# Hybrid encoder layer on one core: the merge-gate columns of the long sequence with seven block products in place of eight, block sums kept in DRAM

## The chip, the cores and the metric

One NeuronCore of a Trainium2 chip runs the whole program in one launch. The metric is the device time in microseconds (us) of that core; lower is better. All tensors are float32. Every matrix product is done in split form: an operand x is written as hi + lo in the chip's float32r type, and a product is three matmuls, hi·hi, hi·lo and lo·hi.

## The reference

Two sequences, 1024 tokens (called 0 below) and 2048 tokens (called 1), of width 1024 pass through one encoder layer; 16 learned meta tokens stand ahead of each.

```python
xn = _rmsnorm(h, g_pre)
proj = xn @ w_in + b_in                    # 1024 -> 6672 columns
na_q, na_k, na_v, na_z, ml_qk, ml_v, ml_z, ml_o, ml_g, mg = jnp.split(proj, SPLIT_IDX, axis=-1)
ya = (neighbourhood_attention(na_q, na_k, na_v, na_rpb) * silu(na_z)) @ w_a
yb = (mlstm_branch(ml_qk, ml_v, ml_g, ml_o, ...) * silu(ml_z)) @ w_b
ga, gb = jnp.split(jax.nn.sigmoid(mg), 2, axis=-1)
y = (ga * ya + gb * yb) @ w_out
return h + _rmsnorm(y, g_post)
```

The change is about `mg`, the last 2048 of the 6672 columns: `sigmoid(xn @ w_in[:, 4624:6672] + b)`.

## The kernel before, in words

**Two streams of work on one TensorE.** `dense` is a generator that yields the big products one small piece at a time, each with its cost; `sparse` is a generator for the mLSTM (`ml`) and the neighbourhood attention (`na`). `run` steps `sparse` and, between its steps, as many pieces of `dense` as the step's number says. TensorE's instruction order is just the order in which Python emits it; the order on the other engines and on the DMA-issuing queue (SyncE, SP) is made by a scheduler at build time. All engines run their own list strictly in order.

**The dense plan.** `PLAN` lists groups (sequence, first token, columns). A group covers 1024 tokens as two halves of 512. Letters: "m" the mLSTM columns, "n" the attention columns, "g" the 16 merge-gate column blocks of 128; ("f", s, b) are the final products. The order is 0m, 0n, 1m at token 0, 1m and 1n at 1024, 1n at 0, then the gates 1g at 0, 1g at 1024, 0g, then six finals. `sparse` runs ml 0, na 0, ml 1, na 1; ml 0 waits until group 0m is done.

**Columns with the weights stationary (`fm_half`).** For one column block of 128 and one half of 512 tokens, 8 k-blocks times three matmuls (`mm3`, lines 170 to 172) of 128x512 go into one PSUM bank of the ring "pj" (three banks). ScalarE and VectorE then read the bank (`fm_evac`; the gates are a tanh, line 530) into a buffer of the ring "st" (four buffers), and a DMA stores it to DRAM. The z columns of "m" take two "st" buffers each (lines 526 to 528). `tm_unit` (lines 607 to 609) does value columns with the tokens stationary.

**Weights.** `wload` brings a raw weight unit of 512 KB (`wraw`, line 242); `wpump` splits it into `whi` and `wlo` (lines 264, 265; four buffers each), and `wflush` stores both parts to DRAM (line 285), from where they come back when the same columns are needed again (line 257).

**x.** The split x of a half (`xh`, `xl`, two buffers each, 4 MB of DMA for both) is built from a transposed copy of the input; halves of sequence 1 that are needed again later are written to DRAM (`xkeep`, `xput`, one 256 KB piece on every fourth turn of `beside`) and reloaded. For sequence 0 the gates group builds x once more.

**The start of the mLSTM (`ml_gates`).** The mLSTM's own gates (`g_t`, loaded from DRAM, line 975) go through a dozen small VectorE and ScalarE steps, ending in `g_lf` (line 995); TensorE then multiplies `g_lf` by a triangle of ones (line 1001). In TensorE's order this stands a little after the last column of group 0m.

Of the kernel before, what the change touches and what calls it, by code (L numbers as in the profile page):

```python
# [40 lines left out]
PLAN = ((0, 0, "m"), (0, 0, "n"), (1, 0, "m"), (1, 1024, "m"), (1, 1024, "n"), (1, 0, "n"), (1, 0, "g"), (1, 1024, "g"), (0, 0, "g"), ("f", 0, 0), ("f", 0, 1), ("f", 1, 0), ("f", 1, 1), ("f", 1, 2), ("f", 1, 3))  # L41
STEPS = (("ml", 0, ()), ("na", 0, (0, 1)), ("ml", 1, ()), ("na", 1, (0, 1, 2, 3)))
# [11 lines left out]
def _weight_units():  # L54

    return ([("i", x, P) for x in FM_COLS] + [("t", *c, a) for c in TM_COLS for a in range(2)]
            + [("m", f, P) for f in range(KT)] + [("o", c, a) for c in range(4) for a in range(2)])

# [63 lines left out]
class K:  # L122
# [3 lines left out]
    def __init__(self, tc, ins, outs):  # L126
# [8 lines left out]
        self.hold, self.early = deque(), True  # L135

# [55 lines left out]
    def gain(self, name):  # L192

        g = self.wp.tile([P, D], F32, name="gain", bufs=1)
        self.nc.sync.dma_start(g, _bc(self.i[name], 0, D))
        return g
# [37 lines left out]
    def wload(self, most=2):  # L234

        while self.wreq and sum(x[1] is not None for x in self.wraw) < most:
            key, src, nk, w = self.wreq.popleft()
            raw = None
            if key not in self.wseen:
                self.wseen.add(key)  # L240
                raw = self.wrp[0].tile([P, 4 * WU], F32, name="wraw", bufs=self.wrp[1])
                self.nc.sync.dma_start(raw[:, :nk * w], src)
            self.wraw.append((key, raw, nk, w))

    def wpump(self, most=NBW, parts=1, copy=None):
# [4 lines left out]
        while self.wraw and self.wout < most:  # L250
# [3 lines left out]
            lo = wp.tile([P, 4 * WU], F32R, name="wlo", bufs=NBW)  # L254
            if raw is None:
# [43 lines left out]
    def rsum(self, xs, res, first=None):  # L299
# [7 lines left out]
        for q, (xr, n) in todo:  # L307
            junk = wp.tile([P, D], mybir.dt.bfloat16, name="xsq", tag="thT", bufs=1)
# [53 lines left out]
    def opening(self, xp):  # L362
# [17 lines left out]
        self.xnext = [self.xtload(0, 512, e, wp, 4) for e in (0, 1)]  # L380
        self.wload(4)
        self.xnext += [self.xtload(0, 512, e, wp, 4) for e in (2, 3)]
# [17 lines left out]
        self.rr = wp.tile([P, 2, 512], F32, name="rr", tag="gain", bufs=1)  # L400
        self.rm = cp.tile([P, NM], F32, name="rm")
        dt = wp.tile([P, HALF], F32, name="dt", tag="thT", bufs=1)
# [5 lines left out]
        self.wrp = wp, 2  # L408
# [9 lines left out]
        self.rwait[0, 0] = rows  # L418

    def build_half(self, s, t0, res):  # L420
# [13 lines left out]
        if s == 0:  # L434
            xts = self.xnext or [self.xtload(s, t0, e, wp, 4) for e in range(4)]
# [6 lines left out]
            if not self.done:  # L442
                p = self.psum("sm", [P, 512])
                nc.tensor.matmul(p[:, :KT], self.ident, g, start=True, stop=True)
                g = self.cp.tile([P, KT], F32, name="gx")
                nc.vector.tensor_copy(g, p[:, :KT])
            x, r = self.xparts(), []
            for e in range(4):
                self.xsplit(x, xts[e], e, 0, g)
                if not self.done:  # L450
                    self.wflush(2)
                yield
            res.append(tuple(x))
            if self.done:
                return
# [4 lines left out]
            def rows():  # L460
                self.rrows(dg, self.rr[:, 1], "sm")
                self.xp.close()
            self.rwait[s, t0] = rows
        else:
            toks, r = self.tokens(s, t0, range(4), wp, 4), []
# [3 lines left out]
            xts = [self.xtload(s, t0, e, wp, 4) for e in range(3)]  # L469
            yield  # L470
            rr = wp.tile([P, 512], F32, name="rx", tag="thT", bufs=1)
            self.rrows(dg, rr, "pj")
            xts.append(self.xtload(s, t0, 3, wp, 4))
# [16 lines left out]
    def xkeep(self, s, t0, x):  # L490
        where = [j for j, g in enumerate(PLAN) if g[:2] == (s, t0 // 1024 * 1024)]
        if where[-1] - where[0] >= len(where):
            self.xkept[s, t0] = []
            for x, part in zip(x, "hl"):
                d = self.dp.tile([P, KT, 512], F32, name=f"x{part}{s}_{t0}")
                self.xput.extend((d[:, k, :], x[:, k, :512].bitcast(F32)) for k in range(KT))
                self.xkept[s, t0].append(d)

    def beside(self):

        self.turn += 1
        if self.xput and self.turn % 4 == 1:
            self.nc.sync.dma_start(*self.xput.popleft())

# [48 lines left out]
    def fm_half(self, col, w, x, s, t0, meta, done=None, tags=None, late=None):  # L553
# [10 lines left out]
        for j, (q, k) in enumerate(order):  # L564
            c0, c1 = chunks[q]
            if q == len(ps):
                ps.append(self.psum("pj", [P, 512]))
            self.mm3(ps[q][:, :c1 - c0], w[0][:, k, :], w[1][:, k, :], x[0][:, k, c0:c1], x[1][:, k, c0:c1],
                     start=k == 0, stop=k == KT - 1)
# [12 lines left out]
    def tm_unit(self, col, halves, wd):  # L582
        nc, wp = self.nc, self.wp
        ws = self.wtake(2)
        bb = wp.tile([P, WU], F32, name="bb", bufs=2)
# [7 lines left out]
        for j, (x, s, c, n, cnt, tok) in enumerate(todo):  # L593
            st = wp.tile([P, 2, WU], F32, name="stT", bufs=4)
# [81 lines left out]

    def requests(self):
# [3 lines left out]
        for j, (s, t0, cols) in enumerate(PLAN):  # L681
# [3 lines left out]
            else:  # L685
                keys = []
                for kind, c in self.layout(cols):
                    if j >= 5 and ahead:
                        keys.append(ahead.popleft())
                    keys += [("i", x, P) for x in c] if kind == "fm" else [("t", *c, a) for a in range(2)]  # L690
            for k in keys:
                nk, w = (KT, P) if k[0] in "im" else (4, k[2] if k[0] == "t" else 256)
# [17 lines left out]

    def group(self, s, t0, meta, cols, reuse, nxt):
# [3 lines left out]
        nb = None  # L715
        for j, (kind, c) in enumerate(jobs):
            if kind == "tm":
# [3 lines left out]
                continue  # L721
            ws = self.wtake(len(c))
            last = j == len(jobs) - 1
# [357 lines left out]
    def conv_load(self, mp, src, c0, n, T):  # L1081
# [3 lines left out]
        raw = mp.tile([P, BL + 2], F32, name="raw", bufs=3)  # L1085
# [22 lines left out]
    def ml(self, s):  # L1108
# [3 lines left out]
        with tc.tile_pool(name=f"mg{s}", bufs=1, side="right", reuse_waits="tile") as keep:  # L1112
            with tc.tile_pool(name=f"mt{s}", bufs=1, side="right", reuse_waits="tile") as mp:
                self.tri = keep.tile([P, 2, P], F32, name="tri")
                nc.sync.dma_start(self.tri, self.i["tri"])
                self.trim = keep.tile([P, 2, CB, P], F32, name="trim")
                for j in range(CB):
                    nc.sync.dma_start(self.trim[:, :, j, :], self.i["trimask"])
                g = []
                yield from self.ml_gates(s, keep, mp, g)  # L1120
            with tc.tile_pool(name=f"ml{s}", bufs=1, side="right", reuse_waits="tile") as mp:
                self.vas = [mp.tile([P, CB, 130], F32, name=f"va{j}") for j in range(3)]
# [32 lines left out]
    def ml_states(self, mp, s, h, g, NB, sts):  # L1155
# [17 lines left out]
        def conv_b(i):  # L1173
            if i < N:
                n, c0 = seq[i]
                th, c = next(convs.pop(i))
                kf = mp.tile([P, BL], F32, name="kf", bufs=3)
# [29 lines left out]
        for i in range(N):  # L1207
# [7 lines left out]
            kth = mp.tile([P, CB, P], F32R, name="kth", tag="kh", bufs=2)  # L1215
            ktl = mp.tile([P, CB, P], F32R, name="ktl", tag="kl", bufs=2)
# [590 lines left out]
```

## Time and profile before

| | |
|---|---|
| time, median of 3 runs | 2741.05 us (2740.09 to 2742.14) |
| the profiled execution: its time, its span | 2741.18 us, 2739.3 us |
| granted TensorE clock | 0.998 |
| TensorE (PE) busy | 2721.4 us, 99% |
| VectorE (DVE), ScalarE (ACT) busy | 65%, 49% |
| DMA | 660.22 MB, mean 241 GB/s |

PE is the matmul side of TensorE, PEld its weight loads, DVE VectorE, ACT ScalarE, SP the queue that issues nearly all DMAs. In the profile the 512-wide matmuls overlap, so a matmul's own duration is longer than the step from one start to the next. A row of the strip view is one digit for each fortieth of the span, about 68.5 us.

### The profile page before, as it was taken

To read this page: it belongs to the slowest core of one execution; us is meant where nothing else is said; L and a number is where in the kernel's file an instruction comes from. 1 tells how busy PE (TensorE), PEld (TensorE's weight loads), DVE (VectorE), ACT (ScalarE), POOL (GpSimd) and SP (SyncE) were. 2 spreads that over 40 slices of the span, in tenths; PEclk is the share of its full clock that TensorE was granted. 3 is DMA by queue.
4 is the path that set the end of the run, shared out by engine and by line. 5 is a ranking of instruction groups with operands and counts; after the bars stand their busy time and mean duration, and the time that the engine had idled before them with its cause. 6 is when DMAs were issued, how large, how long until landed. Compare 5 with 4: busy or idle time off the path is not lost.

```text
span 2739.3 us, 46935 instructions
## 1 busy us (share of the span) xinstructions
PE 2721.4 (99%) x16312; PEld 2399.3 (88%) x16312; DVE 1785.8 (65%) x5042; ACT 1340.8 (49%) x3236; POOL 16.0 (1%) x104
## 2 busy tenths in 40 slices
PE   9999999999999999999999999999999999999998
PEld 7998898899889988978988888888888989989898
DVE  5332688765556655457768667575668798897854
ACT  6212546543454454256456655563555655555521
POOL 0000000000000000000000000000000000000000
PEclk9999999999999999999999999999999999999999
DMA  9644768855875544596766688576559798988965
GB/s 371 243 163 171 253 209 318 283 182 171 322 242 162 168 142 147 179 320 206 266 234 229 243 306 286 196 235 226 186 191 303 234 327 271 330 282 280 323 233 208
DMA packets 362046, 660.22 MB, mean 241 GB/s; under 512 B 46704, under 2 KB 176448, under 8 KB 361808
## 3 DMA queue, kind: packets, MB, share of 16 engines
q1 hardware_dynamic: 360688, 654.52, 70.9%
q0 software_dynamic: 1120, 2.69, 0.5%
q8 instruction: 129, 2.11, 0.3%
q14 instruction: 109, 0.89, 0.1%
HBM read 454.85 MB, written 202.22 MB: 240 GB/s over the span
## 4 chain that ended last, share of the span: by engine, by line
PE 94%; DMA 3%; DVE 1%; ACT 1%; issue 0%; SPq 0%; DVEq 0%; ACTq 0%
PE pj L170 19%; PE pj L172 19%; PE pj L171 19%; PE pj L607 5%; PE pj L608 5%; PE pj L609 5%; PE pj L1587 3%; PE pj L1589 3%; PE pj L1588 3%; PE sm L941 3%; PE tr L926 3%; DMA wraw<-wu 1%; PE sm L172 1%; PE sm L171 1%; PE sm L170 1%; PE sc L894 1%
## 5 line engine op out<-in xcount | busy, mean ns | idle before, releaser
L170 PE MATMUL pj<-xh,whi 128*128 128x512 f32 (+1 forms) x1984 | 782.3, 394 | 0.4 <-ACT whi L264 0.3
L171 PE MATMUL pj<-xl,whi 128*128 128x512 f32 (+1 forms) x1984 | 764.4, 385 | 0.1
L172 PE MATMUL pj<-xh,wlo 128*128 128x512 f32 (+1 forms) x1984 | 764.2, 385 | 0.2 <-DVE wlo L265 0.2
L172 PEld LDWEIGHTS pj<-xh,wlo 128*128 128x128 f32 x1984 | 373.4, 188 | 80.5 <-DVE wlo L265 0.4
L170 PEld LDWEIGHTS pj<-xh,whi 128*128 128x128 f32 x1984 | 373.4, 188 | 67.0 <-ACT whi L264 1.2
L171 PEld LDWEIGHTS pj<-xl,whi 128*128 128x128 f32 x1984 | 374.0, 189 | 64.3 <-issue 1.0
L607 PE MATMUL pj<-whi,xh 128*128 128x256 f32 (+1 forms) x1152 | 329.0, 286 | 0.0
L608 PE MATMUL pj<-wlo,xh 128*128 128x256 f32 (+1 forms) x1152 | 324.8, 282 | 0.0
L609 PE MATMUL pj<-whi,xl 128*128 128x256 f32 (+1 forms) x1152 | 324.6, 282 | 0.0
L1587 PE MATMUL pj<-whi,mh 128*128 128x256 f32 x768 | 220.0, 286 | 0.6 <-DMA whi<-wh 0.6
L607 PEld LDWEIGHTS pj<-whi,xh 128*128 128x128 f32 x1152 | 217.2, 189 | 0.2
L608 PEld LDWEIGHTS pj<-wlo,xh 128*128 128x128 f32 x1152 | 217.0, 188 | 0.1
L609 PEld LDWEIGHTS pj<-whi,xl 128*128 128x128 f32 x1152 | 216.9, 188 | 0.0
L1589 PE MATMUL pj<-whi,mlo 128*128 128x256 f32 x768 | 216.4, 282 | 0.0
L1588 PE MATMUL pj<-wlo,mh 128*128 128x256 f32 x768 | 216.2, 281 | 0.0
L933 DVE TENSOR_TENSOR pts<-tr,pts 96x384 fp32r<-96x384 f32 (+2 forms) x192 | 119.0, 620 | 83.4 <-ACT pts L928 82.0
L928 ACT ACTIVATE pts<-tr 96x384 fp32r<-96x384 f32 (+2 forms) x192 | 103.6, 539 | 127.6 <-PE tr L926 126.7
L170 PE MATMUL pj<-yh,whi 128*128 128x512 f32 x384 | 154.3, 402 | 0.0
L171 PE MATMUL pj<-yl,whi 128*128 128x512 f32 x384 | 151.2, 394 | 0.7 <-DVE yl L1489 0.7
L172 PE MATMUL pj<-yh,wlo 128*128 128x512 f32 x384 | 151.8, 395 | 0.0
L1587 PEld LDWEIGHTS pj<-whi,mh 128*128 128x128 f32 x768 | 145.2, 189 | 1.7 <-DMA whi<-wh 0.8
L1588 PEld LDWEIGHTS pj<-wlo,mh 128*128 128x128 f32 x768 | 145.2, 189 | 0.9
(290 smaller groups left out, 4972.3 us busy)
## 6 DMA issues: line engine op xcount, KB each, us to landing
whi<-wh SPq DMA_DIRECT2D x192, 512.0 KB
wlo<-wl SPq DMA_DIRECT2D x192, 512.0 KB
wraw<-wu SPq DMA_DIRECT2D x64, 512.0 KB
wh<-whi SPq DMA_DIRECT2D x64, 512.0 KB
wl<-wlo SPq DMA_DIRECT2D x64, 512.0 KB
gt<-st SPq DMA_DIRECT2D x96, 256.0 KB
tg<-gt SPq DMA_DIRECT2D x96, 256.0 KB
xt<-xt SPq DMA_DIRECT2D x32, 512.0 KB
```

The costliest lines, as they stand in the source:

```text
L170: mm(out, ah, bh, start=start, stop=False)
L171: mm(out, ah, bl, start=False, stop=False)
L172: mm(out, al, bh, start=False, stop=stop)
L607: nc.tensor.matmul(o, xh, wh, start=k == 0, stop=False)
L608: nc.tensor.matmul(o, xh, wl, start=False, stop=False)
L609: nc.tensor.matmul(o, xl, wh, start=False, stop=k == KT - 1)
L926: nc.tensor.transpose(pt[:ks, ch, :], pr_[:, ch * ks:(ch + 1) * ks], self.ident)
L928: nc.scalar.activation(pts[:ks, :nb, 0, :], pt[:ks, :nb], AF.Copy)
L933: self.nc.vector.tensor_tensor(pts[:ks, :nb, 1, :], pt[:ks, :nb], pts[:ks, :nb, 0, :].bitcast(F32), op=ALU.subtract)
L1587: nc.tensor.matmul(o, mh[:, k, xs], wh, start=clear > 0 and k == 0, stop=False)
L1588: nc.tensor.matmul(o, mh[:, k, xs], wl, start=False, stop=False)
L1589: nc.tensor.matmul(o, ml[:, k, xs], wh, start=False, stop=clear < 2 and k == KT - 1)
```

## The change

For sequence 1 the gates are computed as a 2x2 block product: two column blocks (a pair) by two halves of tokens, over the even and the odd k-blocks. Winograd's form of Strassen's scheme needs seven block products, where the plain way has eight. One block product is 4 k-blocks times three matmuls of 128x512, so a pair costs 84 matmuls, where the plain way costs 96. It is used for all 8 pairs of group 1g at token 0 and for 7 of 8 pairs at token 1024; the first pair there ("lead") and all of sequence 0 stay plain.

- **Weights (`wprep`)**: in group 0m, beside the products, the 16 raw gate units are loaded, four sums are made for each pair, and 8 operands are split and stored to DRAM: 8 pairs x 8 operands x 512 KB. Their SBUF (pool "pq") lies where ml's first pool goes next, and the group's end runs `wprep` out. A product's weights come back as one operand of 512 KB (hi and lo).
- **x (`tprep`)**: in the two groups 1n four token-block sums are made, split and stored to DRAM, 8 MB for each group; three come back into their own SBUF tiles (`tload`; room is made by closing the pool "bp" and opening "gp"), the fourth over the even k-blocks of the second half's x.
- **Products (`sgates`)**: three PSUM banks A, E, R hold the partial sums; ScalarE copies bank to bank, VectorE adds twice for each pair.
- x of sequence 0 is now also written to DRAM in group 0m and reloaded for its gates. The row factors `rr` go to DRAM and back.
- The prefetch of the final weights starts two groups earlier.
- In `ml` some buffers shrink: `raw` and `kf` from 3 to 2, `kh` and `kl` from 2 to 1, `va` from 3 to 2; `s1` shares a buffer with `th`.

```diff
+SW = ((1, 0), (1, 1024))
...
     def beside(self):
         self.turn += 1
-        if self.xput and self.turn % 4 == 1:
+        if self.xput and self.turn % 4 == 1 and self.turn > 48:
             self.nc.sync.dma_start(*self.xput.popleft())
+        if self.side and self.turn % self.pace == 0 and next(self.side, "end") == "end":
+            self.side = None
...
+    def wprep(self):
+        with self.tc.tile_pool(name="pq", bufs=1, side="right", reuse_waits="tile") as pool:
...
+            for p in range(8):
+                raw = raws.pop(p)
+                sm = pool.tile([P, 4, 512], F32, name="ps", bufs=1)
+                todo = [((p, "11"), (p, "12"), raw[:, 0]), ((p, "21"), (p, "22"), raw[:, 1]),
+                        ((p, "s1"), (p, "s2"), sm[:, 0:2]), ((p, "s3"), (p, "s4"), sm[:, 2:4])]
+                for n, (a, b, x) in enumerate(todo):
+                    o = pool.tile([P, 2, 2, 512], F32R, name="po", bufs=3)
+                    nc.scalar.activation(o[:, :, 0], x, AF.Copy)
+                    nc.vector.tensor_tensor(o[:, :, 1], x, o[:, :, 0].bitcast(F32), op=ALU.subtract)
+                    for q, key in enumerate((a, b)):
+                        self.qd[key] = self.dp.tile([P, D], F32, name=f"q{p}{key[1]}")
+                        nc.sync.dma_start(self.qd[key][:, :], o[:, q].rearrange("p a c -> p (a c)").bitcast(F32))
+                    yield
...
+    def sgates(self, s, t0, lead, nxt):
+        for hf in range(2):
+            if hf == 0:
+                ws = [self.wtake(1)[0] for _ in range(2 * len(lead))]
+            for (p, f), w in zip([(p, f) for p in lead for f in range(2)], ws):
+                yield from self.fm_half(C_GA + (2 * p + f) * P, w, self.xs[hf], s, t0 + 512 * hf, False, done=self.wdone if hf else None)
+        pairs = [p for p in range(8) if p not in lead]
+        self.tload(s, t0, (0,))
...
+            if i == 0:
+                yield from prod(A, "11", True)
+                nc.scalar.activation(E, A, AF.Copy)
+            yield from prod(A, "12", False)
+            if end and nxt:
+                nx = [self.xload(*nxt)]
+            yield from prod(E, "s2", False)
+            out(2 * p, 0, new(), A)
+            yield from prod(R, "s3", True)
+            nc.scalar.activation(A, E, AF.Copy)
+            u7 = new()
+            nc.scalar.activation(u7, R, AF.Copy)
+            for op in ("22", "s1") if i == 0 else ("s1", "22"):
+                yield from prod(A if op == "22" else E, op, False)
+            c22, c21 = new(), new()
+            nc.vector.tensor_tensor(c22, E, u7, op=ALU.add)
+            out(2 * p + 1, 1, c22, c22)
+            nc.vector.tensor_tensor(c21, A, u7, op=ALU.add)
+            out(2 * p + 1, 0, c21, c21)
+            if not end:
+                yield from prod(R, "11", True)
+                nc.scalar.activation(A, R, AF.Copy)
+            yield from prod(E, "s4", False)
+            out(2 * p, 1, new(), E)
+            A, E, R = R, A, E
...
     def group(self, s, t0, meta, cols, reuse, nxt):
...
+            if last and sw:
+                self.drain()
+                self.gopen()
+                self.tload(s, t0, (1, 2, 3))
...
     def dense(self, ctx):
...
+            if cols == "g" and (s, t0) in SW:
+                if not same[0]:
+                    self.xs.append(self.xload(s, t0 + 512))
+                    self.tload(s, t0, (1, 2, 3))
+                for cost in self.sgates(s, t0, self.lead(j), nxt and nxt[:2]):
+                    yield cost
+                    self.beside()
...
+            else:
+                yield from self.group(s, t0, meta, cols, same[0], nxt)
+                if self.side:
+                    self.drain()
```

More of the change, by code (lines that the diff above doesn't have):

```diff
@@ L238, in wload @@
             raw = None
-            if key not in self.wseen:
+            if key[0] != "q" and key not in self.wseen:
                 self.wseen.add(key)
@@ L434, in build_half @@
         if s == 0:
[L435 removed]
+            xts = self.xnext
             self.xnext = None
@@ L441, in build_half @@
             g = self.gpre
[L442 to L446, printed above, removed]
+            p = self.psum("sm", [P, 512])
+            nc.tensor.matmul(p[:, :KT], self.ident, g, start=True, stop=True)
+            g = self.cp.tile([P, KT], F32, name="gx")
+            nc.vector.tensor_copy(g, p[:, :KT])
             x, r = self.xparts(), []
```

253 lines of the change are left out of this document (208 added, 45 removed).

## The prediction, on record before the changed kernel was run

> **What bounds the kernel now.** First the page: the span, the busy shares, and the strips of the DMA engines.
>
> ```profile
> span 2739.3 us, 46935 instructions
> PE 2721.4 (99%) x16312; PEld 2399.3 (88%) x16312; DVE 1785.8 (65%) x5042; ACT 1340.8 (49%) x3236; POOL 16.0 (1%) x104
> ...
> DMA  9644768855875544596766688576559798988965
> GB/s 371 243 163 171 253 209 318 283 182 171 322 242 162 168 142 147 179 320 206 266 234 229 243 306 286 196 235 226 186 191 303 234 327 271 330 282 280 323 233 208
> ```
>
> TensorE is busy 99% of the span, everything else much less; the DMA engines are full in the first fortieth (9 tenths, 371 GB/s) and have room after it. "Busy" alone does not say that TensorE never waits, so next the chronological list of its instructions, in the gate stage, and the view of who waited for whom, for TensorE.
>
> ```profile
> 1499.81 0.40 PE L170 MATMUL pj<-xh,whi 128*128 128x512 f32 x1
> ...
> 1500.97 0.39 PE L172 MATMUL pj<-xh,wlo 128*128 128x512 f32 x1
> ```
>
> ```profile
> PE sm L170 <- ACT kth L1217: 3.4, 2, 1.9
> PE sm L171 <- DVE v L1321: 1.9, 2, 1.3
> ```
>
> Five steps lie between the two matmuls: (1500.97 - 1499.81)/5 = 0.232 us for each 128x512 matmul, start to start. The waits are the two longest entries: 3.4 us in two times. So the kernel is TensorE's list of matmuls, end to end. A matmul taken out is worth 0.232 us, and any new wait of TensorE is paid in full, as no slack stands anywhere to absorb it.
>
> **What is taken out.** A pair of column blocks costs 7 x 12 = 84 matmuls of 128x512, where it cost 96; 8 pairs at token 0 and 7 at token 1024 make 15 x 12 = 180 fewer. 180 x 0.232 = 41.8 us. Nothing is added on TensorE. This term is sure.
>
> **What is added in group 0m: 50 MB of DMA where the engines were half full.** In stretches of the first 290 us (columns: stretch, its length, busy us of PE, PEld, DVE, ACT, POOL, granted clock, DMA share, GB/s):
>
> ```profile
> 0.00:20.00 20.00, 18.43 (x102) 14.03 (x103) 11.23 (x26) 14.26 (x26) 0.74 (x10) 1.00 0.88 327
> 20.00:40.00 20.00, 19.92 (x134) 17.78 (x133) 13.09 (x43) 14.95 (x30) 0.10 (x1) 1.00 1.02 410
> 40.00:60.00 20.00, 20.00 (x86) 15.90 (x85) 9.85 (x23) 9.67 (x15) 0.50 (x8) 1.00 1.00 362
> 60.00:80.00 20.00, 20.00 (x88) 16.15 (x87) 6.15 (x20) 7.94 (x15) 0.47 (x9) 1.00 0.95 374
> 80.00:130.00 50.00, 50.00 (x327) 45.86 (x326) 18.50 (x26) 14.99 (x20) 0.00 (x0) 1.00 0.60 205
> 130.00:180.00 50.00, 50.00 (x421) 50.00 (x420) 15.63 (x32) 9.43 (x15) 0.00 (x0) 1.00 0.53 177
> 180.00:230.00 50.00, 50.00 (x392) 48.68 (x391) 11.72 (x25) 7.73 (x13) 0.00 (x0) 1.00 0.44 154
> 230.00:290.00 60.00, 59.65 (x266) 46.88 (x265) 23.80 (x65) 21.11 (x43) 0.10 (x1) 1.00 0.60 213
> ```
>
> When full, the engines move 362 to 410 GB/s; 374 at a share of 0.95 makes 395, which I take. `wprep` loads 16 units of 512 KB and stores 64 operands of 512 KB (8.4 + 33.6 MB), and x of sequence 0 is written out (8.4 MB). In the built program SP's list up to the last operand store has 288 transfers with 114.5 MB. At 395 GB/s these take 290 us, and 3 us more for the slow first stretch (327 in place of 395 for 20 us).
>
> Who waits for that? ml's first pool lies where "pq" was, so one of its first loads waits for the last operand stores, and `g_t` stands behind it on SP, which works strictly in order. TensorE's first use is L1001:
>
> ```profile
> L975 SPq DMA_DIRECT2D g_t<-gg x2: 405/416/428, 158.4 to 1119.9; - x2
> ...
> 167.63 0.22 DVE L995 TENSOR_TENSOR g_lf<-g_lf,g_e 128x72 f32<-128x72 f32 x1
> ...
> L1001 PE MATMUL sm<-g_lf,tri x8: 195/275/279, 262.0 to 1129.9; 128*128 128x36 f32 x4, 128*128 128x68 f32 x4
> ```
>
> Before, `g_t` is issued at 158.4, `g_lf` is ready at 167.8 (9.4 us later) and TensorE comes to it at 262.0: 94 us of slack. After, TensorE's list up to this point is the same, but `g_lf` is ready at 290 + 3 + 9 = 302. TensorE stands **40 us** late there, however the wait is shared out on the way. At 410 GB/s it is 27 (279 + 9.4 - 262), at 362 it is 64 (316 + 9.4 - 262, plus 1).
>
> Most of it should show much earlier, by the "st" buffers:
>
> ```profile
> 62.47 2.17 SPq L537 DMA_DIRECT2D mq<-st  x3
> ...
> 69.48 0.69 ACT L526 ACTIVATE st<-pj,bfm 128x512 f32<-128x512 f32 x1 [2.89 <-DMA mq<-st]
> ```
>
> Already now the first evacuation of the z columns waits 2.9 us for a store of an earlier "st" buffer. In SP's list that store (the first mq of the second half) is at 24.9 MB; in the new list it is at 37.1 MB. 12.2 MB / 395 GB/s = 31 us later, so the evacuation comes at about 100. ScalarE is in order too: everything behind it waits, the operand splits of `wprep` among it, which need one of three "po" buffers whose stores are in the same backlog. TensorE has three "pj" banks: with 24 x 0.232 = 5.6 us for a column and half it runs on to about 75 and then stops for some 24 us, at the fourth z column. The rest of the 40 comes at L1001.
>
> [...]
>
> `wprep`'s own instructions cost nothing:
>
> ```profile
> L265 DVE TENSOR_TENSOR wlo<-wraw,whi 128x1024 fp32r<-128x1024 f32 x61 | 74.5, 1222 | 42.8 <-ACT whi L264 33.8 <-PE sm L329 4.3 <-PE sm L1377 2.7
> L264 ACT ACTIVATE whi<-wraw 128x1024 fp32r<-128x1024 f32 x61 | 64.5, 1060 | 90.5 <-PE pj L171 50.2 <-PE pj L609 26.1 <-DMA wraw<-wu 10.6
> L1554 DVE TENSOR_TENSOR tg<-tg 128x512 f32<-128x512 f32 x48 | 32.8, 683 | 0.5
> ```
>
> 32 splits and 32 sums make 32 x 1.22 + 32 x 0.68 = 61 us of VectorE and 34 us of ScalarE, in a stage where VectorE is busy 46 of 150 us (80 to 230). 16 splits of gate weights go away later. `tprep` is 31 us of VectorE in each group 1n (12 operations of 1.22 and 24 of 0.68 for four parts), with 8 MB of stores: covered as well; where it is not, up to 5 us each.
>
> **The gate stage.** Rows: the tanh of the gates, and two stretches of the stage.
>
> ```profile
> L530 ACT ACTIVATE st<-pj,bfh x96: 667/687/692, 1433.4 to 2068.3; 128x512 f32<-128x512 f32 x96
> ...
> 1433.00:1640.00 207.00, 207.00 (x1036) 173.30 (x1035) 148.77 (x484) 122.47 (x314) 0.70 (x6) 1.00 0.74 258
> 1640.00:1860.00 220.00, 219.35 (x1098) 183.39 (x1097) 151.06 (x500) 125.15 (x330) 0.20 (x2) 1.00 0.71 244
> ```
>
> 96 halves of 24 x 0.232 us are 535 of the 635 us between the first and the last tanh: the share of dense work is 0.84. A product needs 512 KB of weights per 2.8 us of TensorE, where a plain block had 1 MB per 11.1 (or 1.5 MB with raw load and store in the first group). In the built programs the SP bytes of the first gates group go from 59 to 63 MB, of the second from 46 to 61 MB; with 7/8 of the time that is about 0.9 of the engines. So on average they hold, except at the seam between the groups. There the last pair of token 0 is followed by the lead pair of token 1024, whose second half of x can only be loaded when the last product is done, and stands in SP's list behind the first half (4.2 MB), three reloaded sums (6.3 MB), weights, gate stores and ml's loads: 18.6 MB from the start of the first half's load to the piece that TensorE needs first. 18.6 MB / 395 = 47 us. TensorE has 5 products and the lead's two columns to do meanwhile: (5 x 12 + 48) x 0.232 / 0.84 = 29.8 us. It waits **17 us** (16 at 410, 22 at 362; 5 if the sums go out of the way earlier).
>
> The bank copies: each is one ScalarE operation of the size of L530 (0.687 us). All but the first of a group have a product (2.8 us of TensorE) to hide behind; if that cover went, 15 pairs x 0.7 = 10 us. The first stands between "11" and "12" on the same bank: 2 groups x about 1.2 us = **2 us**. ml's smaller buffers still let each load start four or more steps ahead; I take **1 us** for them and `tprep`, 0 to 15 as bounds (below zero nothing, as nothing gets shorter there).
>
> **The sum**, against the profiled execution (2741.18 us; the median of the runs is 2741.05): 2741.2 - 41.8 + 40 + 17 + 2 + 1 = 2759.4, say **2760 us**, slower by 0.7%. A difference under 0.2% (5.5 us) could not be told from none.
>
> **Rivals.**
> - *The matmuls count, the DMA keeps up* (faster). If large rows go out quicker than in any stretch above, or the backlog is worked off beside it, both waits shrink. It decides at 36 us of waits in all; that needs, say, 430 GB/s over the first 266 us (14 us at L1001) and 13 at the seam: 2741.2 - 41.8 + 14 + 13 + 3 = 2729. For it: most new transfers have 4 KB rows. Against: the row of 20 to 40 us is at a share of 1.02 with 410. Chance 0.18, for 2710 to 2735.
> - *Only the start waits*: the seam is covered by what is left in the buffers: 2741.2 - 41.8 + 40 + 3 + 1 = 2743. Against: bytes between the two loads. Chance 0.17.
> - *Waits breed waits*: ml with fewer buffers and VectorE's extra work stall TensorE too (15), and the engines move 362 in place of 395 (24 more at L1001, 5 at the seam): up to 2804. The row of 40 to 60 us is for it, the shares of VectorE are against it. Chance 0.12.
> - *The clock falls.* TensorE at half speed after a long wait: no wait over 1.9 us is in the trace, and the clock is 1.00 in each stretch above, the first with its idle start included. If each of four long waits cost as much as the longest wait seen (1.9 us), 8 us: 2768. Chance 0.05. [...]
>
> The forecast itself, both waits, has 0.48 (2748 to 2785).
>
> **How the numbers follow.** Low end 2722: within the first rival; high end 2792: the middle of the third. What is left out is half of the first rival (0.09) and half of the third (0.06), and some of the spread. Faster by over 0.2%: the first rival, 0.18. Within 0.2%: some half of the second, 0.10. Slower: the rest, 0.72.
>
> **What would show it.** Right: DMA share 0.95 or more from 20 to 290 us; a wait of over 15 us of TensorE between 70 and 110 us with ScalarE idle "<-DMA mq<-st" ahead of L526's counterpart; `g_t` issued near 290 and L1001's counterpart at 295 to 310; TensorE waiting for `xh` or `xl` some 17 us at the seam; 180 fewer matmuls. Wrong: a DMA rate over 420 GB/s in the first 250 us, L1001's counterpart before 285, or a seam without a wait; the error of the sum is then in that term.

## The result, and the profile after

The changed kernel takes 2818.05 us (median of 6 runs, 2814.24 to 2824.64); the kernel before, beside it, 2741.27 us. The ratio is 1.0281, 95% interval 1.0268 to 1.0295: 77 us slower, where the prediction had 2760 us in a range of 2722 to 2792. The profiled execution has a span of 2814.2 us, 74.9 us more than before. The page of the changed kernel:

```profile
span 2814.2 us, 47371 instructions
PE 2703.1 (96%) x16132; PEld 2379.4 (85%) x16132; DVE 1887.8 (67%) x5176; ACT 1394.3 (50%) x3305; POOL 16.3 (1%) x100
...
PEclk9899899999999999999999998999999999999989
DMA  9999666966697756479778889888669798998945
```

The 180 matmuls are gone (16312 - 16132), and TensorE is idle for 111 us in place of 18 (the span less the busy time). Who made it wait, longest first:

```profile
PE pj L185 <- ACT st L627: 23.1, 1, 23.1
PE sm L1233 <- DVE g_lf L1227: 16.1, 1, 16.1
PE pj L185 <- DMA xh<-xh: 15.2, 1, 15.2
PE pj L186 <- DMA xl<-xl: 5.1, 1, 5.1
PE pj L185 <- ACT yh L1742: 5.1, 1, 5.1
PE pj L185 <- ACT st L632: 5.0, 2, 4.0
PE sm L1173 <- ACT prb L1141: 4.9, 3, 3.5
PE sc L1574 <- DVE den L1624: 3.7, 1, 3.7
PE tr L1705 <- DVE hb L1700: 3.7, 1, 3.7
```

Before, the longest entry was 3.4 us. Some of these waits also slow what comes behind them: about the 4.0 us wait the granted clock is 0.50, from 59.7 to 66.5 us. The chronological list of TensorE after it (start, duration, and the idle time before):

```profile
61.53 0.79 PE L185 MATMUL pj<-xh,whi 128*128 128x512 f32 x1 [4.00 <-ACT st L632]
62.12 0.63 PE L186 MATMUL pj<-xl,whi 128*128 128x512 f32 x1
...
66.39 0.46 PE L187 MATMUL pj<-xh,wlo 128*128 128x512 f32 x1
```

From the second row to the last shown are ten steps: (66.39 - 62.12) / 10 = 0.427 us each, where the prediction counted 0.232. Ten such steps cost 10 x 0.195, some 2 us.

To put the loss at places, I took for each pair of matmuls that follow each other the step from start to start, less the median step of the same two widths before. The sums by stage (idle: steps over 0.3 us too long; slow: the rest, some 15 of its 16.2 us in stretches where the granted clock is 0.50):

| stage, us of the changed kernel | before | after | more |
|---|---|---|---|
| group 0m and the mLSTM's first gates, 0 to 400 | 8.5 | 59.7 | 51.2 |
| 400 to 760 | 5.5 | 6.7 | 1.2 |
| x and sums of token 1024, 760 to 1150 | 5.7 | 20.4 | 14.7 |
| sums of token 0, 1150 to 1390 | 10.5 | 19.9 | 9.4 |
| first gates group, 1390 to 1640 | 3.0 | 3.8 | 0.8 |
| the seam, 1640 to 1780 | 1.4 | 26.2 | 24.8 |
| 1780 to 2640 | 16.3 | 12.7 | -3.6 |
| the end of the attention, 2640 to 2815 | 1.9 | 19.6 | 17.7 |
| all | 52.8 | 169.0 | 116.2 (100.2 idle, 16.2 slow) |

116.2 - 41.8 = 74.4, against 74.9 measured. The windows that answer to those shown of before (same columns), with one of VectorE's full stretches:

```profile
20.00:40.00 20.00, 20.00 (x137) 18.15 (x136) 13.46 (x44) 14.99 (x32) 0.11 (x1) 1.00 1.03 405
...
60.00:80.00 20.00, 18.47 (x70) 14.82 (x71) 2.07 (x3) 5.05 (x8) 0.15 (x1) 0.84 0.92 324
80.00:130.00 50.00, 26.94 (x110) 21.42 (x109) 26.83 (x44) 21.89 (x30) 0.10 (x1) 0.76 1.02 410
130.00:180.00 50.00, 49.41 (x390) 48.55 (x389) 25.85 (x37) 16.24 (x21) 0.00 (x0) 1.00 1.03 406
180.00:230.00 50.00, 50.00 (x426) 50.00 (x426) 26.85 (x40) 12.03 (x14) 0.00 (x0) 1.00 1.00 375
230.00:290.00 60.00, 60.00 (x362) 53.48 (x361) 30.35 (x43) 21.88 (x28) 0.00 (x0) 1.00 0.96 361
290.00:350.00 60.00, 43.57 (x206) 34.33 (x205) 27.52 (x79) 24.08 (x54) 0.78 (x13) 0.86 0.61 212
...
1300.00:1320.00 20.00, 16.25 (x75) 13.48 (x75) 19.90 (x43) 14.04 (x34) 0.00 (x0) 0.91 0.79 275
```

The DMA engines are busy at 0.92 or more in every stretch from 20 to 290 us. The first long wait of TensorE lies inside, from 80.8 to 103.9 us: ScalarE can't empty a PSUM bank into a buffer "st" until the stores that SP issued at 92.8 us have read it (SP's and ScalarE's lists):

```profile
92.81 4.06 SPq L637 DMA_DIRECT2D mq<-st  x4
...
102.22 0.69 ACT L626 ACTIVATE st<-pj,bfm 128x512 f32<-128x512 f32 x1 [5.64 <-DMA mq<-st]
```

Right behind the full stretch TensorE loses its second block. In SP's list the end of the backlog and the gate loads behind it, and TensorE's first use (from the views of single lines and tiles):

```profile
L564 SPq DMA_DIRECT2D q7s<-po x4: 319/413/1101, 296.7 to 298.9; - x4
...
L1206 SPq DMA_DIRECT2D g_t<-gg x2: 380/402/423, 304.3 to 1185.7; - x2
...
L1233 PE MATMUL sm<-g_lf,tri x8: 221/341/426, 310.9 to 1197.5; 128*128 128x36 f32 x4, 128*128 128x68 f32 x4
```

### The profile page after: what moved, and what is told of

It reads as the page before. It is cut to its first block, busy times and chain, and to the rows that moved or that the text cites. A ratio compares the mean times of both kernels' runs of the same rounds, so it can differ in the third digit from the quotient of the medians.

```text
span 2814.2 us, 47371 instructions
## 1 busy us (share of the span) xinstructions
PE 2703.1 (96%) x16132; PEld 2379.4 (85%) x16132; DVE 1887.8 (67%) x5176; ACT 1394.3 (50%) x3305; POOL 16.3 (1%) x100
## 4 chain that ended last, share of the span: by engine, by line
PE 84%; DMA 10%; DVE 3%; ACT 1%; SPq 1%; issue 1%; DVEq 0%; POOL 0%; ACTq 0%; POOLq 0%
PE pj L185 12%; PE pj L187 12%; PE pj L186 12%; PE pj L707 5%; PE pj L708 5%; PE pj L709 5%; PE pj L890 3%; PE pj L892 3%; PE pj L891 3%; PE pj L1824 3%; PE pj L1826 3%; PE pj L1825 3%; PE sm L1173 3%; PE tr L1158 2%; DMA xl<-xl 1%; DMA xt<-xt 1%
## 5 line engine op out<-in xcount | busy, mean ns | idle before, releaser
L185 PE MATMUL pj<-xh,whi 128*128 128x512 f32 (+1 forms) x1360 | 535.7, 394 | 46.2 <-ACT st L627 23.1
L186 PE MATMUL pj<-xl,whi 128*128 128x512 f32 (+1 forms) x1360 | 523.0, 385 | 5.5 <-DMA xl<-xl 5.1
L187 PE MATMUL pj<-xh,wlo 128*128 128x512 f32 (+1 forms) x1360 | 521.8, 384 | 3.7 <-DMA wlo<-wl 3.4
L185 PEld LDWEIGHTS pj<-xh,whi 128*128 128x128 f32 x1360 | 258.5, 190 | 92.0 <-ACT st L627 23.5
L187 PEld LDWEIGHTS pj<-xh,wlo 128*128 128x128 f32 x1360 | 258.2, 190 | 58.1 <-DMA wlo<-wl 4.7
L186 PEld LDWEIGHTS pj<-xl,whi 128*128 128x128 f32 x1360 | 258.7, 190 | 47.7 <-DMA xl<-xl 5.6
```

What stands on the lines that cost most here:

```text
L185: mm(out, ah, bh, start=start, stop=False)
L186: mm(out, ah, bl, start=False, stop=False)
L187: mm(out, al, bh, start=False, stop=stop)
```

## The experiments

The theory after the result: five waits with five causes, each to be moved by itself: bytes ahead of the st stores, the place of `g_t`, the order of loads at the seam, tprep in the way of others, and a dense stream that runs out before the attention does. The rival: no room in DMA and VectorE, so that a wait taken from one place comes back at the next. "Changed" is the kernel with the change; times are medians.

**Four edits of the source alone.** x of sequence 0 stored later:

```diff
-        if self.xput and self.turn % 4 == 1 and self.turn > 48:
+        if self.xput and self.turn % 4 == 1 and self.done:
...
-        while self.xput:
+        while self.xput and self.done:
```

> x of sequence 0 is written out during group 0n in place of 0m (32 stores of 256 KB, 8.4 MB, leave the list ahead of the mLSTM's start); nothing else differs from the changed kernel. Theory (a backlog of bytes): 8.4 MB / 382 GB/s (the 114.5 MB that took 299.9 us) = 22 us less; the two waits at the start (23.2 us for a st buffer, 16.1 us for g_lf) shrink together from 39 to about 17, g_t is issued near 283 us, and the time falls by 20 to 26 us to 2792 to 2798. Rival (the operand stores of wprep alone hold the st buffers and the gate loads, x is beside them): the waits stay above 34 us and the time falls by less than 6 us.

2814.6 us, a number that tests neither theory: the scheduler, which orders every engine but TensorE, issued these stores as soon as x was there. The first of them (the line covers later stores of sequence 1 too):

```profile
L527 SPq DMA_DIRECT2D xh<-xh x42: 319/447/1347, 43.0 to 804.9; - x42
```

The sums at the seam: `self.tload(s, t0, (1, 2, 3))` moved into `sgates`, behind the lead's first half.

> At the seam between the two gate groups of sequence 1 the three reloaded sums (6.3 MB) are asked for only after the lead pair's first half, so the second half of x stands ahead of them in the DMA list. Theory (order in the list): 6.3 MB / 390 GB/s = 16 us less ahead of x; the waits of 15.2 and 5.1 us for xh and xl at 1720 us go to 5 us in all, the sums come in time or cost up to 4 us, and the time falls by 10 to 16 us to 2802 to 2808. Rival (the engines are full there, the order is indifferent): the wait moves from x to the sums and the time stays within 4 us of 2818.

2813.8 us; TensorE, VectorE, ScalarE and SP have the same lists as in the changed kernel, so again nothing was tested. The 4 us between the two medians are what two builds with the same lists can differ by: a gain of 5 us or less in one run proves nothing by itself. The table's stages differ by 2 us at most between the two.

The interleave: `yield A_NA - 0.06 * s` for `yield A_NA` in `na`.

> In the attention of sequence 1 each step gives 0.06 us less of dense work (1.025 in place of 1.085), so the dense stream lasts longer beside it. Theory (the interleave was balanced for 42 us more of dense matmuls; the dense stream reaches the point where it needs the last attention rows too early, and the last steps run uncovered from 2694 to 2717 us): 520 steps x 0.06 = 31 us of dense work are kept back, the 17 us of waits at 2690 to 2720 fall to about 3, and the time falls by 10 to 15 us to 2803 to 2808. Rival (VectorE and the order of its work bound the end, 0.83 busy there): the waits appear earlier in the attention in place of at its end, and the time stays within 4 us of 2818 or rises.

2809.7 us, 8 us less than the changed kernel and 4 less than the run with the same lists, short of the 10 to 15 of the theory. By the table's measure the end loses some 11 us less, and some 4 us more are lost ahead of it, from 1780 to 2640: a part of the rival is true as well. In the stage from 2640 us the waits of 5.1, 3.5, 1.1 and two of 0.7 us became

```profile
PE pj L185 <- ACT yh L1742: 4.1, 1, 4.1
PE pj L1824 <- DMA whi<-wh: 0.4, 1, 0.4
```

TensorE's order is the source's, so this edit did what it says. The dense stream had become 41.8 us shorter and stood still until the last attention rows came.

The sums on every third turn: `self.side, self.pace = self.tprep(s, t0), 3`.

> The sums of x (tprep) take a step on every third turn in place of every second, in both n groups of sequence 1; the same instructions and bytes. Theory (VectorE is full in those stretches: 19.9 of 20 us busy from 1300 to 1320, 27.4 of 30 from 860 to 890, and the mLSTM's and the attention's chains queue behind the sums): the waits of 8 us at 820 to 880 and 10 us at 1310 to 1365 halve, the time falls by 6 to 10 us to 2808 to 2812. Rival (the 8 MB of stores for each group are what delays, or VectorE is late whatever the pace): the same waits over a longer stretch, the time within 3 us of 2818.

2812.9 us, 1 us less than the run with the same lists, so no gain is shown. The waits at 820 and 1310 us shrank, but one of 13.7 us (for `hb`) came at 1362 us, about where the last job's `drain` emits the remaining steps at once (that link was not tested). A slower pace by itself moves the wait.

**With the order enforced.** A helper queues what it issues behind the last SP instruction of the source:

```diff
+    def behind(self):
+        last = next(x for x in reversed(self.nc.cur_bb.bb.instructions) if x.engine == mybir.EngineType.SP)
+        with self.tc.issue_after(last):
+            yield
...
+            with self.behind():
+                self.nc.sync.dma_start(*self.xput.popleft())
```

> As the run with x of sequence 0 kept in group 0n, but now each of its stores is queued on SP behind what the source has there (in the run before, SP's list had them still at 43 to 77 us, so nothing was tested). In the built list the last operand store is at 108.0 MB in place of 114.5 MB, and the second half's first mq store at 27.4 in place of 37.1 MB. Theory (a backlog of bytes): the wait of 23 us for a st buffer near 100 us goes (9.7 MB / 395 GB/s = 25 us earlier), the one for g_lf grows to about 23 to 27 us, as only 6.5 MB / 382 = 17 us are gained there, and the two together fall from 39 to 22 to 27 us: the time falls by 14 to 19 us to 2799 to 2804. Rival (wprep's own loads and stores alone set the first wait): the first wait stays over 15 us and the time falls by less than 6 us.

2797.7 us, 20 us less, against the rival: 14 at the start by the table's measure (59.7 to 45.8), and 7 from 760 to 1150, which the theory did not have. The first block of waits shrank from 23.1 to 8.4 us, and the one for `g_lf` grew to 18.5:

```profile
PE sm L1241 <- DVE g_lf L1235: 18.5, 1, 18.5
PE pj L192 <- ACT st L635: 8.4, 2, 6.0
```

At the seam, `with self.behind(): self.tload(s, t0, (1, 2, 3))` behind the load of x's second half:

> As the run with x ahead of the reloaded sums at the seam, but now the three sums are queued on SP behind the second half of x (in the run before, SP's list had the same order as the changed kernel's, so nothing was tested). Theory (order in the list): 6.3 MB / 390 GB/s = 16 us less ahead of x; the waits of 15.2 and 5.1 us for xh and xl go to at most 5 us in all, the sums cost up to 4 us, and the time falls by 12 to 18 us to 2800 to 2806. Rival (the engines are full, the order is indifferent): a wait of over 10 us for t1, t2 or weights takes its place, and the time stays within 4 us of 2818.

2802.2 us, 16 us less, as the theory has it. By the table's measure 10 of them are at the seam (26.2 to 16.2) and some 4 at the end, where nothing was edited. Of 15.2 and 5.1 us are left

```profile
PE pj L193 <- DMA xl<-xl: 5.3, 1, 5.3
...
PE pj L192 <- DMA xh<-xh: 1.0, 1, 1.0
```

Six edits together (the two above; `yield 11.0 if s else 31`, which is more dense work behind the loads of `g_t`; 0.10 for 0.06; tprep of token 1024 at pace 4; and `if j >= 3 and ahead and (j, x) != (3, 0)` for the prefetch):

> Six edits together: x of sequence 0 kept in group 0n behind the queue; 20 us more dense work between the loads of g_t and the first use of g_lf (sequence 0); the sums behind x at the seam; 0.10 us less dense work for each attention step of sequence 1 (0.06 alone, and 20 us more for the work that was put ahead); the sums of token 1024 on every fourth turn; no prefetch of final weights in the first job of the group at token 1024. Theory (each wait has its own cause and they add up): -17 at the start, -18 more for g_lf, -16 at the seam, -12 at the end, -4 and -3: about 2748 (2740 to 2756). Rival (a wait that is taken away at one place comes back at the next, as the engines of DMA and VectorE are the bound over the whole span): 2775 or more.

2786.3 us: the rival's side. The 20 us of dense work brought their own weight and store DMAs ahead of `g_t` in SP's list (its load went from 290.5 to 298.7 us against the run with x alone), so 11.3 us of that wait stayed; and waits for `q` (11.3) and `hb` (8.9) of the mLSTM grew. The sum of single gains was not to be had by pushing work ahead.

**Parts left out.** wprep's body replaced by a single `yield`:

> wprep is left out, with its loads, VectorE and ScalarE work and stores; the gate products read other kept weights of the same size in place of its operands, so the gates come out wrong and all else is as in the changed kernel. x of sequence 0 is still written out in group 0m. In SP's list the second half's first mq store is at 35.3 MB (37.1 with wprep, 24.9 before the change). Theory (two waits with two causes: the first at 100 us is the x stores', the one for g_lf is wprep's): the wait for g_lf goes, 16 us and some 2 us of slower clock behind it; the first stays at 17 to 22 us; the time falls by 18 to 25 us to 2793 to 2800. Rival (wprep's work on ScalarE and in the st ring makes the first wait too): the first wait is under 8 us and the time falls by over 35 us.

2790.6 us, 27 us less: the wait for `g_lf` is gone, and 18.6 of the first 23.1 us are still there. So the first belongs in the main to the stores of x, the second to wprep:

```profile
PE pj L185 <- ACT st L594: 18.6, 1, 18.6
PE pj L185 <- DMA xh<-xh: 13.4, 1, 13.4
```

tprep's body left out; and tprep without its stores:

> tprep is left out in both n groups, its VectorE and ScalarE work and its 16 MB of stores; the reloads of the sums read pieces of the kept x of the same size, so the gates come out wrong and all else is as in the changed kernel. Theory (the waits of the mLSTM and the attention at 820 to 880 and at 1310 to 1365 us come from tprep): these 17 us with the clock's part go, the time falls by 13 to 18 us to 2800 to 2805. Rival (they come from the smaller buffers of ml and from the earlier prefetch of the final weights): the time stays within 5 us of 2818.

> tprep works as in the changed kernel on VectorE and ScalarE, but stores nothing (16 MB of stores out); the reloads read pieces of the kept x in their place, so the gates come out wrong. Theory (VectorE's queue is what delays): the waits at 820 to 880 and 1310 to 1365 stay, the time is within 5 us of 2818. Rival (the stores delay other transfers): it falls as far as without tprep, by 13 us or more.

2794.7 and 2812.3 us: 23 and 6 us less than the changed kernel, the second only 1 less than the run with the same lists. The waits from 740 to 1390 us, first without tprep, then without its stores alone:

```profile
PE pj L187 <- DMA wlo<-wl: 3.1, 2, 2.6
PE pj L185 <- DMA whi<-wh: 1.8, 1, 1.8
```

```profile
PE sc L1571 <- DVE q L1525: 7.7, 2, 4.2
PE pj L187 <- DMA wlo<-wl: 2.7, 2, 2.3
```

By the table's measure the stage from 1150 to 1390 goes from 19.9 to 7.5 us without tprep and only to 19.3 without its stores: there tprep's work on VectorE and ScalarE is the cause, not its stores. The stage from 760 to 1150 goes from 20.4 to 14.2 and 13.5. That speaks for the stores, against my theory; but the stage falls as far (13.2 and 14.4) with x of sequence 0 queued behind and without wprep, runs that leave tprep as it is and shift the two streams against each other, so the stores' part there is not shown. Some 8 us at 770 to 790, mostly waits for weights, are in all three kernels; their cause I did not isolate.

**The place of `g_t`.** The first mLSTM's first pools (`mg`, `mt`) are opened ahead of wprep's:

```diff
                 self.xp.close()
+                self.pre = self.gpools(0)
                 self.side, self.pace = self.wprep(), 2
...
-        with tc.tile_pool(name=f"mg{s}", ...) as keep:
-            with tc.tile_pool(name=f"mt{s}", ...) as mp:
+        ks, keep, ms, mp = self.pre or self.gpools(s)
+        with ks:
+            with ms:
```

Tried with other edits first (x behind, sums behind, 0.06, prefetch, and tprep started in the m groups), then alone:

> Six edits together: x of sequence 0 kept in group 0n behind the queue; the first pools of the first mLSTM opened ahead of wprep's, so that g_t, tri and trim no longer lie where the operands were; the sums behind x at the seam; 0.06 us less dense work for each attention step of sequence 1; no prefetch of final weights in the first job at token 1024; tprep moved from the n groups to the m groups of sequence 1 (every third and every fourth turn). Theory (each wait has its own cause): -20, -18 (g_t is loaded near 200 us and g_lf no longer waited for; the next loads of ml wait for the last operand stores, 3 us or less), -16, -8, -2, -8: about 2746 (2738 to 2756). Rival (what is taken from one place comes back at the next): 2768 or more.

> The changed kernel with one edit: the first pools of the first mLSTM (g_t, tri, trim) are opened ahead of wprep's, so that they no longer lie where the operands were. In SP's list g_t's loads move from behind the last operand store (114.5 MB) to 77 and 79.7 MB. The bytes of group 0m are unchanged. Theory (g_t waits only for its place in SBUF): the wait of 16.1 us for g_lf and the slower clock behind it go; the next loads of ml still wait for the last operand stores at 300 us and cost up to 8 us; the time falls by 10 to 18 us to 2800 to 2808. Rival (the DMA backlog itself delays whatever is behind it): a wait of 14 us or more at the first products of the mLSTM's states takes its place, and the time stays within 5 us of 2818.

2768.9 us together (just on the rival's side, which began at 2768; 14 us of waits at 520 to 560 were new, beside tprep), and 2791.6 us alone, 26 us less, more than the 10 to 18 forecast, though not a byte was saved: `g_t` is loaded at 198.0 us in place of 304.3, `g_lf` isn't waited for any more, and only 2.8 us came back for the mLSTM's first `kf`. By the table's measure the start lost 13 us of its 59.7, as forecast; another 11 us went at 760 to 1390 us, where the edit changes nothing but how the two streams meet, so a part of those waits hangs on a shift of some 16 us. The second wait was one of place; the backlog only set its length.

```profile
L1207 SPq DMA_DIRECT2D g_t<-gg x2: 379/772/1166, 198.0 to 1168.6; - x2
```

**Towards a version without waits.** tprep of token 0 beside the value columns, two lead pairs, 8 us more dense work after `g_t`, 0.08:

> As the run with six edits together, with these differences: tprep for token 0 runs beside the value columns of group 1m (VectorE 0.76 busy from 600 to 640 and 0.61 from 640 to 700 us there, against 0.91 or more from 500 to 580 where it ran), 8 us more dense work after the loads of g_t (the mLSTM's first loads came 6 us late at 300), 0.08 in place of 0.06 us less dense work for each attention step, and two lead pairs in place of one at token 1024 (12 matmuls more, 2.8 us). Theory (each wait is local and is covered by moving work): the 14 us at 520 to 560 fall to 4, the 8 us at 300 go, the seam's 10 us fall to 4, the end's 7 to 4: 2768.9 - 10 - 8 - 6 + 2.8 - 3 = 2745 (2738 to 2752). Rival (DMA and VectorE have too little room in all, what is moved waits elsewhere): 2760 or more.

2763.2 us, the rival's number, but the order was not tested. VectorE's list, too, is the scheduler's: the first sums still ran at 510 us, 90 us ahead of the value columns,

```profile
L597 DVE TENSOR_TENSOR xr<-xh,xl x16: 1204/1217/1226, 510.4 to 863.5; 128x1024 f32<-128x1024 f32 x16
```

so this, too, had to be enforced, with the kernel's own `held`:

```diff
+                with self.held():
                     nc.vector.tensor_tensor(r, h[:, ks, :512]..., l[:, ks, :512]..., op=ALU.add)
...
+        if self.xput and self.turn % (2 if self.turn < 300 else 4) == 1 and self.turn > 216:
```

> The run with tprep beside the value columns, with its order enforced: in that run VectorE's list, which a scheduler makes at build time, still had tprep's first sums at 510 us, 90 us ahead of the value columns, so nothing was moved. Now each first sum is queued behind what the source has on VectorE there; in the built list the sums lie among the value columns' adds. With it x of sequence 0 is stored from the 50th turn of group 0n on, 16 us (in place of 8) more dense work after the loads of g_t, and 0.09 us (0.08) less for each attention step. Theory (local crowding on VectorE): the 22 us of waits at 500 to 600 us go to 5, the 13 us at 320 to 345 to 5: 2763.2 - 17 - 8 = 2738 (2732 to 2748). Rival (too little room on VectorE beside this mLSTM): waits of 12 us or more appear at 600 to 720, and the time is 2754 or more.

2750.0 us: 13 us less, between theory and rival. By the table's measure 11 us went from 400 to 760, where the order was enforced, and 8 at the start, where the later stores of x and the dense work act; some came back behind. So part of it was local crowding; 21 us are left from 380 to 740 us (5.5 before), and whether these are lack of room is open. Then wprep's first raw loads later (four turns, `with self.behind(): load(0); load(1)`), with 22 us and 0.10; and the same with one lead pair:

> The run before this one with the first loads of raw gate weights (2 MB) four turns later and queued behind the last mq stores of group 0m (their last at 29.8 MB of SP's list in place of 31.9), and for that 22 us (in place of 16) more dense work after the loads of g_t and 0.10 us (0.09) less for each attention step. Theory (the waits of 7.3 us for st buffers at 80 and 101 us come from bytes ahead of the stores): 2.1 MB / 395 = 5 us less for each of the two, some 5 us in all, nothing lost at 328 us: 2745 (2741 to 2750). Rival (the waits for st are set by the order on ScalarE, or the 5 us come back at 330 us where the mLSTM's first loads are 5 us later): 2748 or more.

> The same with one lead pair at token 1024 in place of two: 12 matmuls fewer (2.8 us), and 11 us less of plain columns while the second half of x is loaded. Theory (the seam is covered but for 4 us with two): the wait for xl grows by 3 to 6 us, and the time is 0 to 3 us above the run with two leads. Rival (the sums behind x have covered the seam already): it is 2 to 3 us faster.

2744.6 us, as the theory has it, and 2753.8 us. The st waits of 7.3 us are gone to 1.3; and the second lead pair, which costs 2.8 us of matmuls, is worth 9 us, more than either side had: by the table's measure 4 us less are lost at the seam and 6 us less at the end, where the longer dense stream covers more. The longest wait was now 8.7 us at the seam, for the mLSTM's `q`, whose loads stood behind the sums. So these were asked for only after the lead's first half, with the same helper, in `sgates`:

```diff
+            if lead and hf == 0:
+                with self.behind():
+                    self.tload(s, t0, (1, 2, 3))
```

> As the run with the raw weights later and two lead pairs, but the three sums are asked for only after the first half of the lead pairs and queued there, so that 12 loads of the mLSTM (2.1 MB), which stood behind the 6.3 MB of sums, now stand ahead of them. Theory (the wait of 8.9 us at 1686 us for the mLSTM's q is the 6.3 MB of sums ahead of its raw load, 16 us at 390 GB/s): that wait goes, the sums are still in time (22 us of the lead's second half and 5.6 us of two products lie between), and the time falls by 6 to 10 us to 2736 (2733 to 2741), the first below the kernel before. Rival (the DMA engines are full there): the wait moves to the sums or to the weights, and the time is 2743 or more.

2735.6 us (11 runs), 82 us less than the changed kernel, as the theory has it. The ratio to before is 0.9984, interval 0.9975 to 0.9994: some 4 us less than the kernel before, but that is no more than two builds with the same lists differed by, so call the two equal. Its longest waits:

```profile
PE tr L1733 <- DVE hb L1728: 6.2, 2, 4.0
PE tr L1473 <- DVE kf L1437: 5.3, 1, 5.3
```

It does the same block products, with 12 matmuls more for the second lead pair, and still writes and reads all the sums. By the table's measure 91.1 us are lost in place of 52.8; so of the 41.8 - 2.8 = 39 us of matmuls taken out nearly all is still paid in many small waits, and the profiled execution, 2739.67 us, stands above that version's own median.

## Why the prediction was wrong

- **What is taken out**: right, 180 matmuls; the table closes with 41.8 us to within 0.5 us of the measured span.
- **The bytes of group 0m**: right. The last of the 114.5 MB was issued at 298.9 us (293 forecast), 383 GB/s in place of the 395 taken. `g_t` came at 304.3 and TensorE's first use at 310.9 (302 forecast), and the first block near 100 us came at 103.9, 23.1 us long (24 forecast). It was mis-sized by what lies around: 4 us at 61.5, and the slower steps; 51 in place of 40. That the first block is due in the main to x's 8.4 MB, and the other to wprep and the place of `g_t`, the prediction did not separate; the runs did.
- **The seam**: the mechanism was right, 24.8 us in place of 17 (20.3 of them waits for `xh` and `xl`); x stood behind the sums, and putting them behind it took 10 us off there.
- **The bank copies**: 2 us were forecast; the waits for them (`PE pj L890 <- ACT pj L909`) are 0.9 us in two times.
- **The step that failed** is the 1 us for ml's smaller buffers and tprep ("covered as well", 0 to 15). Its stages hold 24 us: 14.7 from 760 to 1150 and 9.4 from 1150 to 1390 us. With tprep left out 6 of the first and 12 of the second go (the second then loses less than before the change); the 8 us at 770 to 790 stay, with their cause open. The cover was read from VectorE's mean share in the stage, and VectorE is not asked for its mean: from 1300 to 1320 it is busy 19.9 of 20 us, and the mLSTM's `den` and `hb` queue behind sums of up to 1.22 us each. How much is lost hangs also on how the streams meet: opening `g_t`'s pool earlier took 11 us off these stages. ml's smaller buffers show next to no loss where the first mLSTM runs without tprep beside it: 1.2 us from 400 to 760.
- **What had no term at all** is the end: 17.7 us. A shorter dense stream meets the attention's last rows sooner; the prediction treated the interleave as given, though its own term of 41.8 us changed it. Less dense work for each attention step took some 11 us off the end. Against the 60 us of waits forecast, the table's 116.2 are 24 more for tprep's term, 18 at the end, 11 at the start and 8 at the seam, less 5 for the bank copies and the stages without a term.
- **The clock**: the rival with 0.05 and 8 us was true, with 16 us, on top of the waits. The text went by stretches in which the clock is 1.00; it did not look behind the wait of 1.9 us at 1381 us in the trace of before. There the granted clock is 0.50 from 1382.3 to 1385.7 us, and the steps are as slow as after the change ((1384.99 - 1382.85) / 5 = 0.428 us):

```profile
1382.85 0.63 PE L170 MATMUL pj<-xh,whi 128*128 128x512 f32 x1
...
1384.99 0.63 PE L172 MATMUL pj<-xh,wlo 128*128 128x512 f32 x1
```

  So a step takes 0.428 us in place of 0.232 for the 3.4 us at 0.50; about the wait of 4.00 us in the changed kernel the clock is at 0.50 for 6.8 us. In these two traces the length of a wait alone does not tell whether the clock falls: it did behind 1.93 us here, while in the changed kernel a wait of 2.6 us at 1342 us left it at 1.00.
- "Waits breed waits" (up to 2804) was the nearest rival, and half of its reason came true: VectorE's extra work did stall TensorE (15 us allowed, some 18 gone with tprep left out), but the engines moved 383 GB/s and not 362. It had neither the end nor the slower steps, so the result, 2818, lies above even its top, and the range ended at 2792, the middle of it.

## What to carry to other kernels

Where one engine is busy 99%, a saving on it can be lost, and more with it, unless every stream that feeds it is followed past the edit: the bytes queued ahead of the next needed load, the pool whose memory the next load takes, and the balance of two streams that share the engine. Cover is a matter of a few microseconds at one place; look at the full stretches of an engine, not at its mean over the stage. And where a scheduler makes the queues, look where an instruction ended up in the list before believing that an edit of the source has moved it.

## What was not expected of the hardware

In the changed kernel the core moved 410 GB/s from 80 to 130 us and 406 from 130 to 180 us, loads and stores together; the prediction took 395. And before the change TensorE's granted clock fell to 0.50 behind a wait of only 1.93 us, whose slower steps (3.4 us of them, each 0.428 us in place of 0.232, so some 1.6 us lost) cost nearly as much again; the wait of 2.6 us at 1342 us of the changed kernel left the clock at 1.00 and cost only itself.
